# Block-diagonal gates, attention values and FFN sums of squares in fp32r passes over high and low parts, with the attention values gathered by block of keys

## The chip, the cores and the metric

The kernel runs on one core of one Trainium2 chip. The time is the device time of one execution in microseconds (us). The profile is one execution seen by the hardware profiler. TensorE appears in it as PE (matmuls) and PEld (its weight loads), VectorE as DVE, ScalarE as ACT, GpSimd as POOL, and SyncE, which issues most transfers, as SP.

## The reference, cut to what matters

A first block (convolution, a gated linear recurrence, stick-breaking attention, an MLP) is followed by two layers of a second block, on 512 positions of 1024 channels. The change is in the second block:

```python
def second_block(x, ...):
    for l in range(2):
        x = x + 0.5 * swiglu(rms_norm_2(x, ffn1_norm[l]), ...)          # 1024 -> 2816 -> 1024
        h = rms_norm_2(x, mix_norm[l])
        proj = h @ w_in[l] + b_in[l]
        q, k, v, f_logit, xr, gr, g_attn, g_rnn = jnp.split(proj, SPLIT_POINTS, axis=-1)
        q, k = rms_norm_2(q, q_norm[l]), rms_norm_2(k, k_norm[l])       # per head, 8 heads of 128
        log_f = jax.nn.log_sigmoid(f_logit)
        y_attn = forgetting_attention(q, k, v, log_f) @ w_o_attn[l]     # causal softmax(q k + c_i - c_j) v
        xr = causal_depthwise_conv(xr, conv_w[l], conv_b[l])            # 4 taps
        yr = rg_lru(xr, lru_w_a[l], lru_b_a[l], lru_w_x[l], lru_b_x[l], lru_lambda[l]) * gelu(gr)
        merged = sigmoid(g_attn) * y_attn + sigmoid(g_rnn) * (yr @ w_o_rnn[l])
        x = x + merged @ w_out[l]
        x = x + 0.5 * swiglu(rms_norm_2(x, ffn2_norm[l]), ...)

def rg_lru(x, w_a, b_a, w_x, b_x, lam):
    r = sigmoid(block_diag_linear(x, w_a, b_a))                         # 16 blocks of 64x64
    i = sigmoid(block_diag_linear(x, w_x, b_x))
    log_a = -8 * r * softplus(-lam); a = exp(log_a)
    u = sqrt(-expm1(2 * log_a)) * (i * x)
    # h_t = a_t h_{t-1} + u_t along the positions
```

## The kernel before, in words

Activations stand as tiles of 128 channels x 512 positions. Each large product is made of three fp32r passes over a high and a low part of both sides (`mm3`, L225 to L229): high x high, high x low, low x high. Weights come in chunks of 256 KB: `w` (L183 to L199) has SP load `raw`, ACT cast it to `hi` (L195) and DVE subtract for `lo` (L196), in rings of four. Sums grow in four PSUM banks, the tiles `a` (pool `pa`, four buffers); a new sum can begin only in a bank that has been read out. Four more banks serve small products: `xs` twice, `xm` and `xh` once each.

Small products use plain fp32 operands, for which PE executes two instructions where the program has one: the block-diagonal gates (L909, L910), the scores (L842), the values (L867) and the sums over partitions for the norms (`rows_of`, L270).

In a layer, `ffn` (L807), `mix` (L961) and `ffn` follow each other. The part of `mix` around the change runs in this order of the program:

- `stats`, and the block-diagonal matrices `bd`, loaded as fp32 (L988 to L995).
- Four pairs of sums give the eight tiles of xr. Each is scaled out of its bank into a tile `t` (L980, DVE) and moved with its bias into `xr` (L1004, ACT).
- `rnn` (L894), for each of eight tiles j: four taps of the convolution into `xc` on DVE (L905, L907); two gates on PE (L909, L910); on ACT tanh, tanh, exp, tanh and a square (L912 to L915, L298); two products on DVE (L918, L917). After j = 3 and after j = 7, ACT takes four square roots (L923) and DVE makes four products and four scans (L925, L926).
- The forget gate: one sum `fa` in an `a` bank (L1009 to L1013), read out by DVE into a tile `s` (L1016); then a softplus on ACT (L957 to L959), a scan, a transfer to DRAM.
- Twice, for half of the heads: the tokens of q, k and v. `tokens` (L255) needs four `a` banks at once, for the four blocks of 128 tokens, and takes each weight chunk through all four. Then `heads_T` (norm and transposes to `qkT`) for q and k, then `attn` (L870), and four tiles of the gelu branch.
- `attn_scores` (L836) makes the softmax rows of one block i of queries of one head in a tile `s`; `attn_values` (L856) transposes them into `xs`, copies to `pT` (L865), and multiplies with v for each block j of keys up to i, 128 columns at a time (L867).

A scheduler sets the order of each engine's instructions ahead of time; on the chip each engine takes its own in that order. Work marked with `hp()` goes ahead when it is ready. Pools give SBUF: a pool opened after another was closed takes the space of that one, and its first writers come behind the last readers of what lay there. Before, one pool `mb` (L966) holds the tiles for all of `mix`:

```python
self.pool(ctx, f"mb{l}", hm=8, t=3, bq=1, qk=5, v=6, qkT=8, cb=2, s=3, pT=2)   # L966
    pool = self.pool(c2, f"rn{l}", bd=4, xc=3, abc=8)                          # L986, closed after rnn
```

Of the kernel before, what the change touches and what calls it, by code (L numbers as in the profile page):

```python
# [7 lines left out]
F32 = mybir.dt.float32  # L8
F32R = mybir.dt.float32r
# [109 lines left out]
class Build:  # L119
# [96 lines left out]
        self.tc.keep_in_program_order(ins)  # L216
        return ins

    def split(self, src, tag):
        hi, lo = self.t(tag, F32R), self.t(tag, F32R)  # L220
        self.nc.scalar.copy(hi, src)
        self.nc.vector.tensor_tensor(lo, src, hi.bitcast(F32), op=OP.subtract)
        return hi, lo
# [42 lines left out]
    def rows_of(self, p, scale, xt="xm"):  # L266
# [4 lines left out]
                                  start=True, stop=True)  # L271
        return ps[:, 0:4]

    def rsqrt(self, src, w, g="m"):

        nc = self.nc
        m, r = self.small(w, g), self.small(w, g)
        nc.vector.tensor_scalar(m, src, EPS, None, op0=OP.add)
        nc.gpsimd.tensor_tensor(r, m, self.mhalf[:, :w], op=OP.pow)
        return r  # L280
# [8 lines left out]
        nc.scalar.copy(rb, ps)  # L289
        return rb  # L290

    def stats(self):
        rt = self.rsqrt(self.rows_of(self.p, 1.0 / D), 4)
        return rt, self.spread(rt)

    def square(self, x, tag="sq"):
# [12 lines left out]
    def setup(self):  # L309
        nc, cp = self.nc, self.cp  # L310
        self.cv = self.lined(cp, (128, NVEC), name="cv")
        with self.hp():
            nc.sync.dma_start(self.cv, self.ap["vecs"])
        cst = self.lined(cp, (128, 384), name="cst")
        nc.scalar.dma_start(cst, self.ap["cst"])
        self.ident = cst[:, 0:128]
        self.ones = {}
        for v, nm in ((1.0, "one"), (1.0 / D, "oned"), (1.0 / 512, "onec"), (1.0 / 128, "onev")):
            o = self.lined(cp, (128, 128 if v in (1.0, 1.0 / 512) else 2), name=nm)
            nc.gpsimd.memset(o, v)  # L320
            self.ones[v] = o
        self.mhalf = self.lined(cp, (128, 32), name="mhalf")
        nc.gpsimd.memset(self.mhalf, -0.5)
        self.cst = cst
# [482 lines left out]
    def ffn(self, n, l, nxt, spill=None):  # L807
        nc = self.nc
        h = self.hx
        with ExitStack() as ctx:  # L810
            self.pool(ctx, f"ffn{n}{l}", act=44, G=4)
            with self.hp():
                _, rb = self.stats()
            acts = []
            for f in range(0, 22, 2):
                accs = self.pairs(*[_cols(f"ffn{n}_w_{v}_2", l, 8, f * 128) for v in ("gate", "up")], h)
                ga, ua = accs[0:2], accs[2:4]
                for i in range(2):
                    with self.hp():
                        G, U = self.t("G"), self.t("G")  # L820
                        nc.vector.tensor_tensor(G, ga[i], rb, op=OP.mult)
                        nc.scalar.activation(G, G, AF.Silu)
                        nc.vector.tensor_tensor(U, ua[i], rb, op=OP.mult)
                        nc.vector.tensor_tensor(U, U, G, op=OP.mult)
                        acts.append(self.split(U, "act"))
            for m in range(0, 8, 2):
                for i, a in enumerate(self.pair(f"ffn{n}_w_down_2", l, 22, m * 128, acts)):
                    with self.hp():
                        x = self.x[m + i]
                        nc.vector.scalar_tensor_tensor(x, a, 0.5, x, op0=OP.mult, op1=OP.add)  # L830
                        if nxt:
                            self.ready(m + i, nxt, spill)
                        else:
                            nc.sync.dma_start(self.ap["oT"][(m + i) * 128:(m + i) * 128 + 128, :], x)
# [18 lines left out]
        nc.vector.tensor_scalar(s, s, ri, None, op0=OP.mult)  # L853
        return st

    def attn_values(self, st, v, vc, i, o):  # L856

        nc = self.nc
        n = (i + 1) * 128
        pt = self.aux("xs")  # L860
        for j in range(i + 1):
            js = slice(j * 128, j * 128 + 128)
            nc.tensor.transpose(pt[:, js], st[:, js], self.ident)  # L863
        pT = self.t("pT")
        nc.scalar.copy(pT[:, :n], pt[:, :n])  # L865
        for j in range(i + 1):
            nc.tensor.matmul(o[:, i * 128:n], v[j][:, vc:vc + 128], pT[:, j * 128:j * 128 + 128],  # L867
                             start=(i == 0 and j == 0), stop=(i == 3 and j == 3), skip_group_check=True)

    def attn(self, qT, kT, v, hd0, ct, cdram):  # L870

        nc = self.nc
        out, todo = [], []

        def values(st, hd, i):
            if i == 0:
                out.append(self.aux("xh"))
            self.attn_values(st, v, (hd - hd0) * 128, i, out[-1])
            if i == 3:
                y = self.t("x")  # L880
                nc.scalar.copy(y, out[-1])
                out[-1] = y

        for hd in range(hd0, hd0 + 4):
            cb = self.t("cb")
            nc.gpsimd.dma_start(cb, cdram[hd:hd + 1, :].to_broadcast([128, 512]))
            for i in range(4):
                todo.append((self.attn_scores(qT[hd - hd0], kT[hd - hd0], i, hd, ct, cb), hd, i))
                if len(todo) > 1:
                    values(*todo.pop(0))  # L890
        values(*todo.pop(0))
        return out

    def rnn(self, xr, bd, l, hb, sp4):  # L894
        nc = self.nc
        hs = []
        for j0 in range(0, 8, 4):
            av, vv, ix = [], [], []
            for j in range(j0, j0 + 4):
                xc = self.t("xc")  # L900
                for tap in range(CW2):
                    wv = self.col(("conv_w_2", l), j * CW2 + tap)
                    src = xr[j][:, tap:tap + 512]
                    if tap == 0:
                        nc.vector.tensor_scalar(xc, src, wv, self.col(("conv_b_2", l), j), op0=OP.mult, op1=OP.add)  # L905
                    else:
                        nc.vector.scalar_tensor_tensor(xc, src, wv, xc, op0=OP.mult, op1=OP.add)  # L907
                ga, gx = self.aux("xs"), self.aux("xs")
                nc.tensor.matmul(ga, bd[0][j // 4][:, j % 4], xc, start=True, stop=True)  # L909
                nc.tensor.matmul(gx, bd[1][j // 4][:, j % 4], xc, start=True, stop=True)  # L910
                ti, th, a = self.t("abc"), self.t("abc"), self.t("hm")
                nc.scalar.activation(th, ga, AF.Tanh, scale=0.5, bias=hb[:, j:j + 1])  # L912
                nc.scalar.activation(ti, gx, AF.Tanh, scale=0.5, bias=hb[:, 8 + j:9 + j])
                nc.scalar.activation(a, th, AF.Exp, scale=sp4[:, 8 + j:9 + j], bias=sp4[:, 8 + j:9 + j])
                nc.scalar.activation(th, th, AF.Tanh, scale=sp4[:, j:j + 1], bias=sp4[:, j:j + 1])  # L915
                a2 = self.square(a, "xc")
                nc.vector.scalar_tensor_tensor(th, a2, 1.0, th, op0=OP.add, op1=OP.mult)  # L917
                nc.vector.scalar_tensor_tensor(ti, ti, 1.0, xc, op0=OP.add, op1=OP.mult)  # L918
                av.append(a)
                vv.append(th)  # L920
                ix.append(ti)
# [39 lines left out]
    def mix(self, l):  # L961
        nc = self.nc
        h = self.hx
        with ExitStack() as ctx:
            lp = ctx.enter_context(self.tc.tile_pool(name=f"lp{l}", bufs=1))
            self.pool(ctx, f"mb{l}", hm=8, t=3, bq=1, qk=5, v=6, qkT=8, cb=2, s=3, pT=2)  # L966
            with self.hp():
                rt, rb = self.stats()
            hb = self.lined(lp, (128, 32), name="hb")
# [13 lines left out]
            ct = self.lined(lp, (128, 32), name="ct")  # L983
            cdram = self.dp.tile([8, 512], F32, name=f"cd{l}")
            with ExitStack() as c2:
                pool = self.pool(c2, f"rn{l}", bd=4, xc=3, abc=8)  # L986
                bd = []
                for nm in ("lru_w_a_2", "lru_w_x_2"):  # L988
                    b = [self.t("bd", shape=(128, 4, 128)) for _ in range(2)]
                    for hh in range(2):  # L990
                        nc.gpsimd.memset(b[hh], 0.0)
                        src = self.ap[nm][l, hh * 8:hh * 8 + 8].rearrange("(j two) c d -> two c j d", two=2)
                        nc.gpsimd.dma_start(b[hh][0:64, :, 0:64], src[0])
                        nc.gpsimd.dma_start(b[hh][64:128, :, 64:128], src[1])
                    bd.append(b)  # L995

                xr = []
                for m in range(0, 8, 2):
# [6 lines left out]
                        xr.append(u)  # L1005
                hs = self.rnn(xr, bd, l, hb, sp4)
                self.tap(f"hs{l}", hs[0])

            fa = self.acc()  # L1009
            for k0 in (0, 4):  # L1010
# [19 lines left out]
            for hf in range(2):  # L1030
                for n in range(3):
# [2 lines left out]
                    nc.gpsimd.dma_start(bq, self.ap["brow"][l:l + 1, c:c + 512].to_broadcast([128, 512]))  # L1034
                    ts = []
                    for tt, a in enumerate(self.tokens("w_in_2", l, c, h)):
                        v = self.t("v" if n == 2 else "qk")
                        with self.hp():
                            nc.vector.scalar_tensor_tensor(v, a, rt[:, tt:tt + 1], bq, op0=OP.mult, op1=OP.add)  # L1039
                        ts.append(v)  # L1040
                    if n == 0:
                        qT = self.heads_T(ts, 4, 128, qg)
                    elif n == 1:
# [142 lines left out]
```

## Time and profile before

| | us |
|---|---|
| median of 3 runs | 3426.9 (3426.14 to 3427.21) |
| the profiled execution's own time | 3427.6 |
| its span, first to last instruction | 3425.8 |
| PE busy with matmuls | 3390.9 |
| DVE busy | 1887.3 |
| ACT busy | 1309.0 |
| POOL busy | 165.2 |

The span is the stretch between the first and the last instruction of the profiled execution; its own time is what that execution is listed with. PE's matmuls are pipelined: a matmul's listed duration is longer than the step from its start to the next one's, and the step is what it costs in a row of matmuls.

### The profile page before, as it was taken

What the parts mean: (1) busy time and instruction counts of PE and PEld (TensorE: products, weight loads), DVE (VectorE), ACT (ScalarE), POOL (GpSimd) and SP (SyncE); (2) the same over time, 40 slices, a digit from 0 to 9 for tenths busy, and PEclk for the clock granted to TensorE, in tenths of its full rate; (3) what the DMA queues carried; (4) which work ended last, traced back from release to release, by engine and by line L of the source; (5) the groups of instructions that cost most, each with busy time, mean ns of one, the idle gap of its engine ahead of it and who ended that gap; (6) DMA issues with size and microseconds to landing.
All of it is one profiled execution on the core that took longest, in us unless ns stands there. A gap on an engine that the chain in (4) does not pass through costs nothing.

```text
span 3425.8 us, 42240 instructions
## 1 busy us (share of the span) xinstructions
PE 3390.9 (99%) x15436; PEld 2777.9 (81%) x15436; DVE 1887.3 (55%) x3164; ACT 1309.0 (38%) x2284; POOL 165.2 (5%) x273
## 2 busy tenths in 40 slices
PE   7999999999999999999999999999999999999999
PEld 6887778788888888788888888888887788888887
DVE  7698565544444434786455444444447865454442
ACT  3335443423333323654433333333336644343331
POOL 0011100000000001111000000000010110000000
PEclk9999999999999999999999999999999999999999
DMA  5223344333333333222333333333342232433332
GB/s 207 74 75 96 103 132 142 116 108 96 98 94 98 98 108 114 91 89 89 111 96 94 98 98 99 95 97 97 104 123 93 90 90 79 122 96 97 98 103 91
DMA packets 184064, 350.79 MB, mean 102 GB/s; under 512 B 21168, under 2 KB 22448, under 8 KB 182832
## 3 DMA queue, kind: packets, MB, share of 16 engines
q1 hardware_dynamic: 177552, 328.53, 31.4%
q0 software_dynamic: 6160, 19.37, 1.8%
q8 instruction: 121, 1.98, 0.2%
q14 instruction: 87, 0.71, 0.1%
q10 hardware_dynamic: 144, 0.20, 0.0%
HBM read 341.69 MB, written 6.32 MB: 102 GB/s over the span
## 4 chain that ended last, share of the span: by engine, by line
PE 97%; DVE 1%; ACT 1%; issue 0%; DMA 0%; POOL 0%; DVEq 0%; ACTq 0%; POOLq 0%
PE a L227 30%; PE a L229 30%; PE a L228 30%; PE xh L867 1%; PE xs L842 1%; PE xh L441 1%; PE xh L523 1%; PE xs L501 1%; PE xs L863 1%; PE xm L404 0%; DVE xc L907 0%; PE xh L517 0%; PE xh L330 0%; PE xh L480 0%; PE xs L909 0%
## 5 line engine op out<-in xcount | busy, mean ns | idle before, releaser
L196 DVE TENSOR_TENSOR lo<-raw,hi 128x512 fp32r<-128x512 f32 x1144 | 786.5, 689 | 1243.3 <-ACT hi L195 1228.9
L195 ACT CAST hi<-raw 128x512 fp32r<-128x512 f32 x1144 | 707.2, 619 | 1592.4 <-PE a L228 1299.1
L227 PE MATMUL a<-h,hi 128*128 128x512 f32 x2528 | 989.3, 393 | 2.3 <-ACT h L601 2.3
L228 PE MATMUL a<-h,hi 128*128 128x512 f32 x2528 | 991.1, 392 | 0.0
L229 PE MATMUL a<-h,lo 128*128 128x512 f32 x2528 | 982.9, 392 | 0.0
L227 PEld LDWEIGHTS a<-h,hi 128*128 128x128 f32 x2528 | 475.8, 188 | 107.4 <-issue 7.5
L229 PEld LDWEIGHTS a<-h,lo 128*128 128x128 f32 x2528 | 475.5, 188 | 103.3 <-issue 5.2
L228 PEld LDWEIGHTS a<-h,hi 128*128 128x128 f32 x2528 | 475.5, 188 | 102.9 <-issue 5.1
L228 PE MATMUL a<-act,hi 128*128 128x512 f32 x960 | 373.6, 389 | 0.0
L227 PE MATMUL a<-act,hi 128*128 128x512 f32 x960 | 373.5, 389 | 0.0
L229 PE MATMUL a<-act,lo 128*128 128x512 f32 x960 | 372.8, 389 | 0.0
L228 PE MATMUL a<-Y,hi 128*128 128x512 f32 x544 | 214.4, 394 | 0.0
L227 PE MATMUL a<-Y,hi 128*128 128x512 f32 x544 | 213.7, 393 | 0.0
L229 PE MATMUL a<-Y,lo 128*128 128x512 f32 x544 | 212.4, 391 | 0.0
L227 PEld LDWEIGHTS a<-act,hi 128*128 128x128 f32 x960 | 180.2, 188 | 37.5
L229 PEld LDWEIGHTS a<-act,lo 128*128 128x128 f32 x960 | 180.2, 188 | 37.4
L228 PEld LDWEIGHTS a<-act,hi 128*128 128x128 f32 x960 | 180.2, 188 | 37.4
L229 PE MATMUL a<-hi,h 128*128 128x512 f32 x512 | 204.3, 402 | 0.0
L228 PE MATMUL a<-lo,h 128*128 128x512 f32 x512 | 203.6, 398 | 0.0
L227 PE MATMUL a<-hi,h 128*128 128x512 f32 x512 | 199.6, 408 | 1.7 <-DVE qk L1039 1.7
L227 PEld LDWEIGHTS a<-Y,hi 128*128 128x128 f32 x544 | 102.1, 188 | 23.0 <-issue 1.6
L228 PEld LDWEIGHTS a<-Y,hi 128*128 128x128 f32 x544 | 102.1, 188 | 22.8 <-issue 1.8
(291 smaller groups left out, 3068.0 us busy)
## 6 DMA issues: line engine op xcount, KB each, us to landing
raw<-in_w_l SPq DMA_DIRECT2D x852, 256.0 KB, 2.6
raw<-in_w_first SPq DMA_DIRECT2D x284, 256.0 KB, 2.6
mr<-in_mod_b_ SPq DMA_DIRECT2D x64, 256.0 KB, 3.2
mq<-in_mod_a SPq DMA_DIRECT2D x8, 1024.0 KB, 8.5
xs<-x POOLq DMA_DIRECT2D x16, 256.0 KB, 2.3
cb<-cd POOLq DMA_DIRECT2D x16, 256.0 KB, 3.5
x<-xs POOLq DMA_DIRECT2D x16, 256.0 KB, 3.6
bq<-in_brow POOLq DMA_DIRECT2D x12, 256.0 KB, 3.8
```

Of the source, the lines that this page charges most:

```text
L195: nc.scalar.copy(hi, raw)
L196: nc.vector.tensor_tensor(lo, raw, hi.bitcast(F32), op=OP.subtract)
L227: mm(acc, w[0], x[0], start=start, stop=False)
L228: mm(acc, w[0], x[1], start=False, stop=False)
L229: mm(acc, w[1], x[0], start=False, stop=stop)
L441: mm(ps[:, i * 64:i * 64 + 64], k[:, s], q[:, s].rearrange("p (n c h) -> p n c h", c=2, h=h)[:, :, 1], start=True, stop=True)
L501: mm(z[:, o:o + n], q[pr, blk(i)], k[pr, :n], start=True, stop=True)
L523: mm(pt[pr, c], v[j][:, hd * 64:hd * 64 + 64], f[:, o + j * 128:o + j * 128 + 128], start=j == 0, stop=j == i, skip_group_check=True)
L842: nc.tensor.matmul(ps[:, :n], qT[:, ts], kT[:, :n], start=True, stop=True)
L863: nc.tensor.transpose(pt[:, js], st[:, js], self.ident)
L867: nc.tensor.matmul(o[:, i * 128:n], v[j][:, vc:vc + 128], pT[:, j * 128:j * 128 + 128], start=(i == 0 and j == 0), stop=(i == 3 and j == 3 ...
```

## The change

- Gates: `xc` is split into a high and a low part `xd` (ACT cast, DVE subtraction), the four `bd` matrices of a layer too, and each fp32 matmul of L909 and L910 is replaced by `mm3`.
- Values: a head's values are made at once, by block j of keys, for all blocks of queries from j on. One `mm3` of 512, 384, 256 and 128 columns takes the place of ten fp32 matmuls of 128 columns. The transposed rows are split into `pT` high and low, and v into high and low. The values of a head stand behind the first two blocks of scores of the next head.
- Sums of squares: in `ffn`, `stats(True)` splits `p` and makes eight fp32r matmuls with two columns for four fp32 ones with one column.
- Pools: `mb` has no `v`, `s` and `pT` any more, `t` goes from 3 to 2 and `cb` from 2 to 1. `rn` gets `bd=8` and `xd=4`. A new pool `at` with `v=8, s=5, pT=2` opens after `rn` has been closed.

```diff
+    def rows_of2(self, p, scale, xt="xm"):
+        hi, lo = self.split(p, "pr")
+        ps = self.aux(xt)
+        for i in range(4):
+            s = slice(i * 128, i * 128 + 128)
+            for n, part in enumerate((hi, lo)):
+                self.nc.tensor.matmul(ps[:, 2 * i:2 * i + 2], part[:, s], self.mean, start=n == 0, stop=n == 1)
+        return ps[:, 0:8:2]
...
-                _, rb = self.stats()
+                _, rb = self.stats(True)
...
-    def attn_values(self, st, v, vc, i, o):
-        n = (i + 1) * 128
-        pt = self.aux("xs")
-        for j in range(i + 1):
+    def attn_values(self, sts, v, vc):
+        o = self.aux("xh")
+        for j in range(4):
             js = slice(j * 128, j * 128 + 128)
-            nc.tensor.transpose(pt[:, js], st[:, js], self.ident)
-        pT = self.t("pT")
-        nc.scalar.copy(pT[:, :n], pt[:, :n])
-        for j in range(i + 1):
-            nc.tensor.matmul(o[:, i * 128:n], v[j][:, vc:vc + 128], pT[:, j * 128:j * 128 + 128],
-                             start=(i == 0 and j == 0), stop=(i == 3 and j == 3), skip_group_check=True)
+            n = 512 - j * 128
+            pt = self.aux("xs")
+            for i in range(j, 4):
+                nc.tensor.transpose(pt[:, (i - j) * 128:(i - j) * 128 + 128], sts[i][:, js], self.ident)
+            hi, lo = self.t("pT", F32R), self.t("pT", F32R)
+            nc.scalar.copy(hi[:, :n], pt[:, :n])
+            nc.vector.tensor_tensor(lo[:, :n], pt[:, :n], hi[:, :n].bitcast(F32), op=OP.subtract)
+            self.mm3(o[:, j * 128:], [a[:, vc:vc + 128] for a in v[j]], (hi[:, :n], lo[:, :n]), j == 0, j == 3)
...
         for hd in range(hd0, hd0 + 4):
+            sts = []
             for i in range(4):
-                todo.append((self.attn_scores(qT[hd - hd0], kT[hd - hd0], i, hd, ct, cb), hd, i))
-                if len(todo) > 1:
-                    values(*todo.pop(0))
-        values(*todo.pop(0))
+                sts.append(self.attn_scores(qT[hd - hd0], kT[hd - hd0], i, hd, ct, cb))
+                if i == 1 and todo:
+                    out.append(self.attn_values(*todo.pop(0)))
+            todo.append((sts, v, (hd - hd0) * 128))
+        out.append(self.attn_values(*todo.pop(0)))
...
                 ga, gx = self.aux("xs"), self.aux("xs")
-                nc.tensor.matmul(ga, bd[0][j // 4][:, j % 4], xc, start=True, stop=True)
-                nc.tensor.matmul(gx, bd[1][j // 4][:, j % 4], xc, start=True, stop=True)
+                xd = self.split(xc, "xd")
+                for g, b in ((ga, bd[0][j // 4]), (gx, bd[1][j // 4])):
+                    self.mm3(g, [v[:, j % 4] for v in b], xd, True, True)
...
-            self.pool(ctx, f"mb{l}", hm=8, t=3, bq=1, qk=5, v=6, qkT=8, cb=2, s=3, pT=2)
+            self.pool(ctx, f"mb{l}", hm=8, t=2, bq=1, qk=5, qkT=8, cb=1)
...
-                pool = self.pool(c2, f"rn{l}", bd=4, xc=3, abc=8)
+                pool = self.pool(c2, f"rn{l}", bd=8, xc=3, xd=4, abc=8)
...
-                    b = [self.t("bd", shape=(128, 4, 128)) for _ in range(2)]
+                    b = [self.t("abc", shape=(128, 4, 128)) for _ in range(2)]
...
-                    bd.append(b)
+                    bd.append([self.split(v, "bd", (128, 4, 128)) for v in b])
...
                 hs = self.rnn(xr, bd, l, hb, sp4)
                 self.tap(f"hs{l}", hs[0])
+            self.pool(ctx, f"at{l}", v=8, s=5, pT=2)
...
-                        v = self.t("v" if n == 2 else "qk")
+                        v = self.t("qk")
...
-                        ts.append(v)
+                            ts.append(self.split(v, "v") if n == 2 else v)
```

The change also moves instructions. The first place is PE in `mix` of the first layer, around the gates (`xs` are the banks of the gates, `a` those of the large sums, `xc` the convolved tile, `xd` its parts, `hi` and `lo` a weight chunk). Before, around the gates of j = 1 (L909, L910):

```order
L228 MATMUL a2441_11386<-lo2452_11428,h2199_10297 128x512
L229 MATMUL a2441_11386<-hi2451_11427,h2200_10298 128x512
L909 MATMUL xs2380_11168<-xc2379_11163,bd2296_10791 128x512
L910 MATMUL xs2381_11169<-xc2379_11163,bd2298_10799 128x512
L227 MATMUL a2440_11385<-hi2454_11445,h2203_10308 128x512
L227 MATMUL a2442_11387<-hi2445_11391,h2156_10075 128x512
```

With the change, from the last pass into `a2468`, the third bank of q, through what is left of the gates of j = 2 and the start of those of j = 3:

```order
L229 MATMUL a2468_11480<-hi2480_11538,h2206_10319 128x512
L228 MATMUL xs2401_11230<-xd2404_11233,bd2300_10809 128x512
L229 MATMUL xs2401_11230<-xd2403_11232,bd2301_10810 128x512
L228 MATMUL xs2402_11231<-xd2404_11233,bd2306_10825 128x512
L229 MATMUL xs2402_11231<-xd2403_11232,bd2307_10826 128x512
L227 MATMUL xs2410_11258<-xd2412_11260,bd2300_10809 128x512
L227 MATMUL xs2411_11259<-xd2412_11260,bd2306_10825 128x512
L228 MATMUL xs2410_11258<-xd2413_11261,bd2300_10809 128x512
```

and from the last gates, those of j = 7, to the next large sum:

```order
L227 MATMUL xs2446_11382<-xd2448_11384,bd2302_10813 128x512
L227 MATMUL xs2447_11383<-xd2448_11384,bd2308_10829 128x512
L228 MATMUL xs2446_11382<-xd2449_11385,bd2302_10813 128x512
L229 MATMUL xs2446_11382<-xd2448_11384,bd2303_10814 128x512
L228 MATMUL xs2447_11383<-xd2449_11385,bd2308_10829 128x512
L229 MATMUL xs2447_11383<-xd2448_11384,bd2309_10830 128x512
L227 MATMUL a2469_11481<-hi2471_11484,h2158_10085 128x512
```

Between the gates of j = 0 and those of j = 7 there stood 306 large passes and transposes of q and k; now there stand 60: 24 into the bank of `fa` and 12 into each of three banks of q. Of these, 36 come before the gates of j = 1, 12 between the parts of j = 1 and 12 between those of j = 2. From there to `a2469`, the fourth bank of q, PE has nothing but gates. The second layer has the same order.

The second place is DVE in the same stretch. Before, L1016 reads `fa` out right behind the convolution of j = 1:

```order
L196 TENSOR_TENSOR lo2452_11428<-raw2450_11425,hi2451_11427 128x512
L907 SCALAR_TENSOR_TENSOR xc2379_11163<-xr2317_10888,cv_72,xc2379_11163 128x512
L1016 TENSOR_TENSOR s2435_11365<-a2428_11328,rb2295_10778 8x512
L196 TENSOR_TENSOR lo2455_11446<-raw2453_11443,hi2454_11445 128x512
L980 TENSOR_TENSOR t2370_11138<-a2355_11060,rb2295_10778 128x512
```

With the change the same instruction is L1027, and it stands behind the last scan (now L936) of j = 7:

```order
L935 TENSOR_TENSOR abc2450_11394<-abc2450_11394,abc2451_11395 128x512
L936 SCALAR_TENSOR_TENSOR hm2443_11368<-hm2443_11368,abc2441_11366 128x512
L936 SCALAR_TENSOR_TENSOR hm2452_11396<-hm2452_11396,abc2450_11394 128x512
L1027 TENSOR_TENSOR s2461_11458<-a2454_11421,rb2297_10788 8x512
L1030 TENSOR_SCALAR s2461_11458<-s2461_11458,cv_72 8x512
L1031 TENSOR_TENSOR s2461_11458<-s2461_11458,s2462_11459 8x512
L196 TENSOR_TENSOR lo2484_11557<-raw2482_11554,hi2483_11556 128x512
```

Its tile `s` lies in the pool `at`, and so in the space of `rn`. `lo2484` is the fifth weight chunk of q; the chunk before it, `lo2481`, stands 62 rows earlier, and up to L1027 all rows between are of `rnn` but the two that read out the last two tiles of xr. On ACT the high part `hi2483` stands behind the softplus.

## Rows read from the trace of the kernel before

**Rows 1.** The page's first part: busy us (share of the span) and instructions of each engine.

```profile
span 3425.8 us, 42240 instructions
PE 3390.9 (99%) x15436; PEld 2777.9 (81%) x15436; DVE 1887.3 (55%) x3164; ACT 1309.0 (38%) x2284; POOL 165.2 (5%) x273
```

**Rows 2.** The waits, PE: line waited for, us in total, times, longest.

```profile
PE a L227 <- DVE qk L1039: 1.7, 2, 0.9
PE xm L404 <- ACT qkT L406: 0.8, 2, 0.4
```

**Rows 3.** Timeline of PE, first layer: start us, us, instruction, count.

```profile
1360.08 0.39 PE L229 MATMUL a<-h,lo 128*128 128x512 f32 x1
...
1361.44 0.39 PE L229 MATMUL a<-h,lo 128*128 128x512 f32 x1
...
1363.03 1.02 PE L909 MATMUL xs<-xc,bd 128*128 128x512 f32 x2
1363.89 1.02 PE L910 MATMUL xs<-xc,bd 128*128 128x512 f32 x2
1364.35 0.79 PE L227 MATMUL a<-h,hi 128*128 128x512 f32 x1
1364.98 0.40 PE L228 MATMUL a<-h,hi 128*128 128x512 f32 x1
```

**Rows 4.** Timeline of PE, values of one block of queries and scores.

```profile
1491.57 1.05 PE L867 MATMUL xh<-pT,v 128*128 128x128 f32 x8
1492.46 0.27 PE L863 MATMUL xs<-cst,s 128*128 128x128 f32 x1
1492.57 0.81 PE L842 MATMUL xs<-qkT,qkT 128*128 128x384 f32 x2
```

**Rows 5.** Timeline of all engines, sums of squares ahead of an `ffn`.

```profile
960.30 0.69 DVE L306 TENSOR_TENSOR p<-p,sq 128x512 f32<-128x512 f32 x1
...
965.34 0.95 PE L270 MATMUL xm<-oned,p 128*128 128x1 f32 x8
```

**Rows 6.** Page, costliest groups: DVE's subtraction and ACT's cast (busy, mean ns).

```profile
L196 DVE TENSOR_TENSOR lo<-raw,hi 128x512 fp32r<-128x512 f32 x1144 | 786.5, 689 | 1243.3 <-ACT hi L195 1228.9
L195 ACT CAST hi<-raw 128x512 fp32r<-128x512 f32 x1144 | 707.2, 619 | 1592.4 <-PE a L228 1299.1
```

**Rows 7.** Timeline of DVE in `rnn`, first layer.

```profile
1367.52 0.69 DVE L918 SCALAR_TENSOR_TENSOR abc<-abc,xc 128x512 f32<-128x512 f32 x1 [2.71 <-ACT abc L913]
...
1390.05 0.69 DVE L918 SCALAR_TENSOR_TENSOR abc<-abc,xc 128x512 f32<-128x512 f32 x1 [1.83 <-ACT abc L913]
1390.66 0.74 DVE L907 SCALAR_TENSOR_TENSOR xc<-xr,cv,xc 128x512 f32<-128x512 f32 x1
1391.32 0.69 DVE L917 SCALAR_TENSOR_TENSOR abc<-xc,abc 128x512 f32<-128x512 f32 x1
1391.92 0.75 DVE L907 SCALAR_TENSOR_TENSOR xc<-xr,cv,xc 128x512 f32<-128x512 f32 x1
...
1406.02 1.22 DVE L926 TENSOR_TENSOR_SCAN hm<-hm,abc 128x512 f32<-128x512 f32 x1
1407.15 0.67 DVE L925 TENSOR_TENSOR abc<-abc,abc 128x512 f32<-128x512 f32 x1
```

**Rows 8.** Timeline of ACT, first layer: softplus, gates of one tile, square roots.

```profile
1372.12 0.71 ACT L957 ACTIVATE s<-s,cv 8x512 f32<-8x512 f32 x1
...
1374.80 0.63 ACT L959 ACTIVATE s<-s 8x512 f32<-8x512 f32 x1
...
1387.91 0.69 ACT L912 ACTIVATE abc<-xs,hb 128x512 f32<-128x512 f32 x1 [0.87 <-PE xs L909]
...
1401.59 1.28 ACT L923 ACT_TABLE_LOAD   x1
1402.88 2.20 ACT L923 ACTIVATE abc<-abc 128x512 f32<-128x512 f32 x4
```

**Rows 9.** Windows: us; busy us of PE, PEld, DVE, ACT, POOL; granted clock; DMA.

```profile
600.00:609.00 9.00, 5.35 (x16) 3.99 (x17) 4.99 (x9) 3.24 (x5) 1.03 (x1) 0.50 0.17 64
1460.00:1540.00 80.00, 80.00 (x403) 66.04 (x403) 63.35 (x130) 41.69 (x90) 12.76 (x18) 1.00 0.30 93
```

More of the change, by code (lines that the diff above doesn't have):

```diff
@@ L217, in pin, with split @@
         return ins
-    def split(self, src, tag):
-        hi, lo = self.t(tag, F32R), self.t(tag, F32R)
+    def split(self, src, tag, shape=(128, 512)):
+        hi, lo = self.t(tag, F32R, shape), self.t(tag, F32R, shape)
         self.nc.scalar.copy(hi, src)
@@ L290, in spread, with stats @@
         return rb
-    def stats(self):
-        rt = self.rsqrt(self.rows_of(self.p, 1.0 / D), 4)
+    def stats(self, two=False):
+        rows = self.rows_of2 if two else self.rows_of
+        rt = self.rsqrt(rows(self.p, 1.0 / D), 4)
         return rt, self.spread(rt)
@@ L321, in setup @@
             self.ones[v] = o
+        self.mean = self.lined(cp, (128, 2), F32R, name="mean")
+        nc.scalar.copy(self.mean, self.ones[1.0 / D][:, 0:2])
         self.mhalf = self.lined(cp, (128, 32), name="mhalf")
@@ L810, in ffn @@
         with ExitStack() as ctx:
-            self.pool(ctx, f"ffn{n}{l}", act=44, G=4)
+            self.pool(ctx, f"ffn{n}{l}", act=44, G=4, pr=2)
             with self.hp():
-                _, rb = self.stats()
+                _, rb = self.stats(True)
             acts = []
@@ L854, in attn_scores @@
         return st
-    def attn_values(self, st, v, vc, i, o):
+    def attn_values(self, sts, v, vc):
         nc = self.nc
-        n = (i + 1) * 128
-        pt = self.aux("xs")
-        for j in range(i + 1):
+        o = self.aux("xh")
+        for j in range(4):
             js = slice(j * 128, j * 128 + 128)
-            nc.tensor.transpose(pt[:, js], st[:, js], self.ident)
-        pT = self.t("pT")
-        nc.scalar.copy(pT[:, :n], pt[:, :n])
-        for j in range(i + 1):
-            nc.tensor.matmul(o[:, i * 128:n], v[j][:, vc:vc + 128], pT[:, j * 128:j * 128 + 128],
-                             start=(i == 0 and j == 0), stop=(i == 3 and j == 3), skip_group_check=True)
+            n = 512 - j * 128
[6 more added lines that the diff above has]
+            self.mm3(o[:, j * 128:], [a[:, vc:vc + 128] for a in v[j]], (hi[:, :n], lo[:, :n]), j == 0, j == 3)
+        y = self.t("x")
+        nc.scalar.copy(y, o)
+        return y
     def attn(self, qT, kT, v, hd0, ct, cdram):
@@ L873, in attn @@
         out, todo = [], []
[L875 to L882, printed above, removed]
         for hd in range(hd0, hd0 + 4):
```

## The prediction

> **What bounds the kernel now.** I read the page's busy times first, then PE's waits, then the timelines of PE, DVE and ACT where the change lies. PE is busy 99% of the span [rows 1], and in `mix` it hardly waits: the two causes there come to 1.7 and 0.8 us over both layers [rows 2]. So two questions decide. What do the exchanged matmuls cost on PE? And does the new order still give PE something to do at every moment? The sum is made against the profiled execution's own 3427.6 us, 0.7 above the median of the runs.
>
> **Gates on PE.** A large fp32r pass of 512 columns costs 0.227 us: from 1360.08 to 1361.44 there are six steps [rows 3]. From the first gate at 1363.03 to 1364.98 there are two fp32 matmuls (four instructions) and one such pass: 1.95 less 0.23 is 1.72, or 0.86 each [rows 3]. Three passes cost 0.68. There are 8 tiles, 2 gates and 2 layers: 32 times 0.18, **5.8 us less**.
>
> **Values on PE.** Eight fp32 instructions of 128 columns take 0.89 us, 0.111 each [rows 4]; a head has twenty, 2.22. No row shows an fp32r pass narrower than 512. The cheap end is in proportion to the columns, but not under 0.111: 0.227, 0.170, 0.114 and 0.111, three times over, 1.87 a head, which saves 5.6 over 16 heads. The dear end is that a narrower pass is no faster than one fp32 instruction: two of 384 columns end 0.65 after the transpose before them, 0.325 each [rows 4], so 0.22 for 256 and 0.11 for 128. With 0.227 for the widest that is 2.64 a head, 6.7 more in all. I take the cheap end, **5.6 less**, since the one width that has a row is cheap, and keep both.
>
> **Sums of squares.** Eight instructions with a weight load each stay eight: 0. The split puts 0.62 and 0.69 [rows 6] between `p` and the sums. Before, `p` is ready at 960.99 and PE takes the sums at 965.34 [rows 5], so 4.3 us of other matmuls cover it. Without that cover it would be 1.3 in each of four `ffn`, 5 in all.
>
> **New work on DVE and ACT.** A layer gets 4 splits of `bd`, 8 of `xc`, 8 of v: 20 casts (12.4 us on ACT) and 20 subtractions (13.8 on DVE) [rows 6]. The low parts of `pT`, 1280 columns a head, are some 1.7 us each, 13.8 for 8 heads. In 1460 to 1540 DVE is busy 63.35 of 80 us [rows 9]; the free 16.6 take up what falls there. I count 0 for v and `pT`, and come back to this below. `xd` is another matter.
>
> **What is moved.** This term is the largest. In the order with the change, `fa` is read out of its bank behind the last scan, since its tile `s` now lies in the space of `rn`. Until then `fa` keeps one of the four banks, and q's tokens need all four. PE has 60 large passes after the gates of j = 0, and then nothing but gates until `a2469`. Four chunks of weights are held by the missing fourth sum, so no later one can be cast either. Undisturbed, PE would get through the 60, the 12 of `a2469` that these chunks allow, and 48 gate passes from 1363.03 in 120 times 0.227, 27.2 us: at 1390.3.
>
> How long `rnn` really takes is read from the steps. From the low part of one `xd` to that of the next:
> - two gate passes, their drain and the start, about 0.8 (0.227 twice, 0.39 less 0.23, two handovers);
> - ACT from its first tanh to the product on DVE: 1387.91 to 1391.32, 3.4 [rows 7, 8], 0.1 to start;
> - that product 0.6 and two taps of 0.66 [rows 7], 1.9;
> - the cast 0.6 and the subtraction 0.7, with 0.1 between.
>
> This makes 7.6 us, in which DVE and ACT mostly wait for each other. Five of the six steps from j = 1 to j = 7 are such. The one from j = 3 to j = 4 holds the square roots: 4.2 to the square, table load and first root 1.9 [rows 8], then four products of 0.6, one tap, three scans of 1.13 [rows 7] and the subtraction: 13.2. After j = 7 the same 6.1, four products and four scans (6.9), and L1016 with 0.7: 13.7. The low part of j = 1 is there by about 1375: the product of j = 0 at 1367.52 [rows 7], then ten steps and a table load. So `fa`'s bank is free at 1375 + 38 + 13.2 + 13.7 = 1440. Then PE has twelve passes, but the fifth chunk is cast only behind the softplus: 3.3 before, with a second table load 4.6 [rows 8], and 0.6 for the cast. PE runs on at about 1445, **55 us late**.
>
> The clock adds to it. At 600 to 609, where PE had waited for the sums of squares, the granted clock was 0.50, the level of 1.2 GHz [rows 9]. In the stall PE is busy 1.4 in 7.6, so I take the lower level: the two passes and the drain of each tile cost 0.6 more (4), and some 1.6 after the stall, as in those 9 us. The Trainium skill (TensorE: Matmul & The Clock Gate, "The HAM clock gate") says the same in its own terms: throttled is the default, and only activity lifts it. By that rule the sum stands; without it each layer would lose 55 and not 60, and the total would be 3524.
>
> **The sum.** 2 times 60, less 5.8, 5.6 and the 2.5 of old waits, is 106 more: 3427.6 + 106 = 3534, or 3533 on the scale of the median.
>
> Its bounds: if DVE never waited in `rnn`, its steps behind 1367.52 would still be 8 of 0.61 (L918), 7 convolutions of 2.44, 27 of 0.6 (L917, L925, the subtractions, xr) and 8 scans of 1.13: 47 us, `fa` free at 1415, PE on at 1420, 30 late. Both layers: 3473. If DVE and ACT took turns throughout, ACT's 42 (8 times 3.4, seven casts, eight roots, three table loads, three tiles of xr) come on top: 72 late, 77 with the clock, and with dear values 3580.
>
> **The rivals.**
> - *The stall is covered* (the other side): `fa` is read out before the scans, or PE has other sums to run. Then the exchange remains: 5.8 + 5.6 less, and 3416. What decides is where L1016 (now L1027) starts: before about 1381, when the 60 passes and the first gates are through, there is no loss. For it: before, it ran at the place of j = 1. Against it: the order of DVE, fixed ahead, has eight scans before it.
> - *DVE alone sets `rnn`'s pace*, and waits overlap better than I think: 30 to 45 late, 3473 to 3505.
> - *DVE becomes the bound in the attention too*: v and `pT` ask for 19.3 us a layer, beside stretches in which DVE is nearly full already; if a quarter to a half of it falls where no cover is, 10 to 20 in all: 3543 to 3553.
> - *The narrow passes are dear*: 12 more, 3545.
>
> **How the numbers follow.** The chain as worked out, alone or with some of the last two: 0.74. DVE's pace: 0.16. Turns throughout, beyond 3570: 0.05. Covered: 0.05. The range 3475 to 3580 takes in the bounds of the stall and of the values and leaves out the covered case and the far ends. A difference of about 0.2%, 7 us, can be told from none. Faster by more: 0.04, the covered case with cheap values; within it: 0.01; slower: 0.95.
>
> **What would show it.** Right: from about 1381 to 1445, and again in the second layer, a stretch of PE with gates alone, 7 to 8 us apart, the granted clock at 0.50, and PE's longest waits on `xd`; the read of `fa` behind the last scan; q's weight casts idle some 60 us. Gates in steps of 0.227 otherwise, and three passes in the values with steps that fall with the columns. Wrong: large passes between the gates of j = 3 to 7, or L1016's successor ahead of the scans; then the time is near 3416. If the tiles follow each other in under 5 us, DVE's pace is the right rival.

## The result and the profile after

The changed kernel takes 3559.8 us (median of 4 runs, 3558.6 to 3562.6) against 3426.5 for the kernel before in the same comparison: ratio 1.039, 95% interval 1.0375 to 1.0406, **133 us more**. 106 more were forecast, 3533, within 3475 to 3580. The profiled execution took 3562.61 us.

The page's first part after, which answers to [rows 1]; PE's granted clock in 40 slices of the span; and what the transfers moved in them:

```profile
span 3559.6 us, 42203 instructions
PE 3413.3 (96%) x15340; PEld 2788.1 (78%) x15340; DVE 1948.5 (55%) x3272; ACT 1338.5 (38%) x2329; POOL 155.6 (4%) x273
...
PEclk9999999999999998899999999999996999999999
...
GB/s 199 72 78 107 96 168 98 122 104 98 95 98 98 102 124 42 71 95 89 107 92 97 96 97 98 95 98 96 109 113 9 107 89 92 107 95 95 99 103 92
```

PE has 96 instructions fewer and is busy 22 us longer, in a span that is 134 longer. No engine's busy time explains this. Two dips do, one in each layer: the transfers fall to 42 and 9 GB/s, and the clock falls with them. PE's waits after (line waited for, us in total, times, longest), where before no cause in `mix` came to more than 1.7 [rows 2]:

```profile
PE xs L227 <- ACT xd L221: 76.8, 12, 7.8
PE a L227 <- DVE s L1027: 24.6, 2, 12.3
...
PE xs L228 <- DVE xd L222: 5.2, 2, 2.6
...
PE a L227 <- ACT Y L221: 2.6, 2, 1.3
```

The timeline of PE after, first layer, of the gates the first high and the first low pass of each tile from the low part of j = 1 on (start us, us, instruction, count, idle time before it and its releaser):

```profile
1377.27 0.39 PE L228 MATMUL xs<-xd,bd 128*128 128x512 f32 x1
...
1384.81 1.22 PE L227 MATMUL xs<-xd,bd 128*128 128x512 f32 x2 [6.47 <-ACT xd L221]
1385.83 0.63 PE L227 MATMUL a<-hi,h 128*128 128x512 f32 x1
...
1389.84 0.39 PE L228 MATMUL xs<-xd,bd 128*128 128x512 f32 x1
...
1397.38 1.22 PE L227 MATMUL xs<-xd,bd 128*128 128x512 f32 x2 [6.47 <-ACT xd L221]
1398.40 0.63 PE L228 MATMUL xs<-xd,bd 128*128 128x512 f32 x1
...
1411.96 0.79 PE L228 MATMUL xs<-xd,bd 128*128 128x512 f32 x1 [2.61 <-DVE xd L222]
...
1421.83 0.63 PE L228 MATMUL xs<-xd,bd 128*128 128x512 f32 x1
...
1430.19 0.63 PE L228 MATMUL xs<-xd,bd 128*128 128x512 f32 x1
...
1438.56 0.63 PE L228 MATMUL xs<-xd,bd 128*128 128x512 f32 x1
...
1452.77 0.80 PE L227 MATMUL a<-hi,h 128*128 128x512 f32 x1 [12.30 <-DVE s L1027]
...
1458.00 1.19 PE L227 MATMUL a<-hi,h 128*128 128x512 f32 x4 [0.31 <-ACT hi L195]
```

This is the stall of the prediction. From 1390 to 1452 PE has nothing but gates (1381 to 1445 was forecast), and a large sum begins again only when L1027 has read `fa` out of its bank. The timeline of DVE after, behind the last gates, shows it behind the last two scans:

```profile
1449.60 2.33 DVE L936 TENSOR_TENSOR_SCAN hm<-hm,abc 128x512 f32<-128x512 f32 x2
1452.04 0.68 DVE L1027 TENSOR_TENSOR s<-a,rb 8x512 f32<-8x512 f32 x1
```

Windows of the stall after (us; busy us of PE, PEld, DVE, ACT, POOL; granted clock; DMA share; GB/s):

```profile
1400.00:1420.00 20.00, 3.60 (x7) 1.66 (x6) 14.57 (x20) 12.07 (x18) 0.10 (x1) 0.50 0.00 0
1420.00:1440.00 20.00, 8.32 (x18) 5.33 (x18) 9.85 (x16) 8.79 (x14) 0.00 (x0) 0.50 0.00 0
1480.00:1600.00 120.00, 119.48 (x559) 97.14 (x558) 84.03 (x163) 57.46 (x108) 14.25 (x21) 1.00 0.33 98
```

The granted clock is at its lower level of 1.2 GHz, and no byte of weights is loaded. DVE and ACT mostly wait for each other: DVE is busy 14.6 and 9.9 of 20 us, ACT 12.1 and 8.8. Behind the stall, PE is busy 119.5 of 120 us at the full clock, and DVE, busy 84, has room in spite of the new work.

### The profile page after: what moved, and what is told of

It reads as the page before. It is cut to its first block, busy times and chain, and to the rows that moved or that the text cites. A ratio compares the mean times of both kernels' runs of the same rounds, so it can differ in the third digit from the quotient of the medians.

```text
span 3559.6 us, 42203 instructions
## 1 busy us (share of the span) xinstructions
PE 3413.3 (96%) x15340; PEld 2788.1 (78%) x15340; DVE 1948.5 (55%) x3272; ACT 1338.5 (38%) x2329; POOL 155.6 (4%) x273
## 4 chain that ended last, share of the span: by engine, by line
PE 95%; DVE 2%; ACT 2%; issue 0%; DMA 0%; POOL 0%; SPq 0%; ACTq 0%; DVEq 0%; POOLq 0%
PE a L227 29%; PE a L228 29%; PE a L229 29%; PE xs L855 1%; PE xh L454 1%; PE xh L536 1%; PE xs L514 1%; DVE xc L916 1%; PE xs L227 1%; PE xs L878 0%; DVE hm L936 0%; PE xm L417 0%; PE xs L228 0%; ACT hm L924 0%; PE xs L229 0%
## 5 line engine op out<-in xcount | busy, mean ns | idle before, releaser
L195 ACT CAST hi<-raw 128x512 fp32r<-128x512 f32 x1144 | 707.7, 619 | 1610.7 <-PE a L228 1248.2
L227 PEld LDWEIGHTS a<-hi,h 128*128 128x128 f32 x512 | 97.5, 192 | 50.2 <-DVE s L1027 26.1
L227 PEld LDWEIGHTS a<-Y,hi 128*128 128x128 f32 x544 | 102.9, 190 | 26.9 <-ACT Y L221 2.9
```

Source lines behind the costliest of these rows:

```text
L195: nc.scalar.copy(hi, raw)
L227: mm(acc, w[0], x[0], start=start, stop=False)
```

## The experiments

Ratios are to the kernel before, timed in the same comparison (3425.3 to 3427.1 us). "Excess" is added up over PE's matmuls in a run's profiled execution: the step from a matmul's start to the next one's, less the usual step of that line and width. It counts waits and steps at the lower clock alike. It is 45 us in the kernel before and 188 after.

| run | us | ratio and interval |
|---|---|---|
| after, `fa` in `qkT` (e1) | 3463.9 | 1.0108 (1.0093 to 1.0123) |
| before, `v`, `s`, `pT` in the late pool (e2) | 3524.5 | 1.0289 (1.0272 to 1.0306) |
| e1, fp32 gates (e3) | 3445.0 | 1.0053 (1.0038 to 1.0068) |
| e1, values as before (e4) | 3479.2 | 1.0155 (1.0139 to 1.0170) |
| e1, `s` by block (e5) | 3465.4 | 1.0113 (1.0098 to 1.0128) |
| e3, `s` by block (e6) | 3447.2 | 1.0060 (1.0045 to 1.0075) |
| e6, `t` 3 and `qk` 4 (e7) | 3454.6 | 1.0083 (1.0066 to 1.0100) |
| e6, fp32 sums of squares (e8) | 3447.0 | 1.0058 (1.0043 to 1.0073) |
| e2, `fa` in `qkT` (e9) | 3452.9 | 1.0077 (1.0060 to 1.0094) |
| e6, `t` 3, one wide `s` (e10) | 3444.9 | 1.0055 (1.0040 to 1.0070) |
| e10, last head ahead (e11) | 3445.9 | 1.0058 (1.0043 to 1.0073) |
| e10, `v` back in `mb`, `pT` by width (e13) | 3425.0 | 0.9995 (0.9986 to 1.0004) |

**The forget gate's tiles outside the space of `rn` (e1).**

```diff
-            fz, fe, fc = [self.t("s")[0:8] for _ in range(3)]
+            fz, fe, fc = [self.t("qkT")[0:8] for _ in range(3)]
```

> The changed kernel, but the three tiles of the forget gate (fz, fe, fc) come from the buffers of qkT, which lie in the pool that is open throughout, and not from the new pool in the space of rnn. Theory A (the forget gate's read-out waits for the end of rnn and so keeps one of the four banks): the stall of some 66 us a layer goes, the exchange of fp32 for three passes shows as 11 us less, the waits near the end of mix (4.6 and 5.8 us) stay or shrink: 3413 to 3425 us. Theory B (the splits load DVE and ACT, and rnn is slow for that, wherever the tile lies): still over 3520. Theory C (two tiles t for three, so that the last sums of xr keep their banks): still over 3520.

Measured 3463.9: 96 of the 133 us come back with one word changed. In the timeline of DVE of this run the read-out stands where it stood before the change, at j = 1:

```profile
1369.33 0.67 DVE L1027 TENSOR_TENSOR qkT<-a,rb 8x512 f32<-8x512 f32 x1
```

The stall with gates alone is gone. But 37 us over the kernel before are left, where the exchange should have shown as a gain.

**The pools alone, with none of the new arithmetic (e2).** On the kernel before:

```diff
-            self.pool(ctx, f"mb{l}", hm=8, t=3, bq=1, qk=5, v=6, qkT=8, cb=2, s=3, pT=2)
+            self.pool(ctx, f"mb{l}", hm=8, t=3, bq=1, qk=5, qkT=8, cb=2)
...
+            self.pool(ctx, f"at{l}", v=6, s=3, pT=2)      # opened after rnn
```

> The kernel before with one edit: v, s and pT are moved from the pool of all of mix into a pool opened after rnn. No splits, no other passes, t stays at 3. Theory A: nearly the whole loss appears without any of the new arithmetic; the steps of rnn lack a cast and a subtraction (1.4 us) but have slower gates, so 45 to 65 us a layer: 3515 to 3560. Theories B and C: within 10 us of 3427.

Measured 3524.5, 97 more than before. The fp32 gates stand in the same stall, and PE waits for the convolution in place of `xd`:

```profile
PE xs L909 <- DVE xc L907: 40.1, 10, 6.4
PE a L227 <- DVE s L1017: 23.2, 2, 11.6
```

So most of the loss is the place of three tags in SBUF.

**Gates in fp32 (e3).** On e1, the gates as before the change, with no split of `xc` and `bd`:

```diff
-                xd = self.split(xc, "xd")
-                for g, b in ((ga, bd[0][j // 4]), (gx, bd[1][j // 4])):
-                    self.mm3(g, [v[:, j % 4] for v in b], xd, True, True)
+                nc.tensor.matmul(ga, bd[0][j // 4][:, j % 4], xc, start=True, stop=True)
+                nc.tensor.matmul(gx, bd[1][j // 4][:, j % 4], xc, start=True, stop=True)
...
```

> As e1_fa_tiles, but the gates stay fp32 matmuls, without the splits of the convolved tile and of the block-diagonal matrices. If the gates' passes are worth what their steps say (0.86 for 0.68 us, 32 times), this is 5.8 us above e1_fa_tiles; if DVE is short of time in rnn there, less than that or even below it.

Measured 3445.0, 19 less than e1, where the passes alone are 5.8 cheaper on PE. In e1 the timeline of PE shows why: ahead of the gates of j = 2 it waits for the cast of `xc` and then runs at half speed, 0.43 a step:

```profile
1382.86 1.22 PE L227 MATMUL xs<-xd,bd 128*128 128x512 f32 x2 [4.90 <-ACT xd L221]
1383.88 0.63 PE L227 MATMUL a<-hi,h 128*128 128x512 f32 x1
1384.31 0.63 PE L228 MATMUL a<-lo,h 128*128 128x512 f32 x1
```

The excess is 92 in e1 and 67 in e3; less the 5.8, that is the 19. Of the 25 some 9 lie here, in both layers together, and some 12 at the end of `mix`, where the last head comes later; the rest is spread over the attention. Why the splits delay the last head was not taken apart.

**Values as before (e4).** On e1, one `attn_values` for each block of queries, with fp32 `v` (L1054 reads v out of its banks straight into `v`):

```diff
...
-            self.pool(ctx, f"at{l}", v=8, s=5, pT=2)
+            self.pool(ctx, f"at{l}", v=6, s=3, pT=2)
...
-                        v = self.t("qk")
+                        v = self.t("v" if n == 2 else "qk")
...
```

> As e1_fa_tiles, but the values are made as before, block by block of queries in fp32, v and the transposed rows unsplit. By their steps the new values are worth about 6 us on PE (2.22 for 1.82 us a head), so this would be 6 above e1_fa_tiles; if the waits near the end of mix (10 us together) come from the last head's values standing late, they go here and it is some 4 below.

Measured 3479.2, 15 above e1, but not because the old values are dear. PE's longest wait in `mix` is a new one, with an excess of 19 and 18 us around it, and the timeline of DVE has the four read-outs of v in one piece, behind the scans:

```profile
PE a L227 <- DVE v L1054: 19.6, 2, 9.8
```
```profile
1478.56 2.73 DVE L1054 SCALAR_TENSOR_TENSOR v<-a,m,bq 128x512 f32<-128x512 f32 x4
```

It is `fa`'s stall once more, now with all four banks. As a price of the values the run is inconclusive. It shows one thing more: PE's wait for `Y` is not among its waits, as it is not in e2, which has the old values too; so that wait comes with the new values.

**Scores by block of queries (e5 on e1, e6 on e3).** At this point I held the five whole `s` to be what makes the last head, and so `Y`, late.

```diff
-        st = self.t("s")
+        st = self.t(f"s{i}", shape=(128, n))
...
-            self.pool(ctx, f"at{l}", v=8, s=5, pT=2)
+            self.pool(ctx, f"at{l}", v=8, s0=2, s1=2, s2=2, s3=2, pT=2)
```

> The changed kernel with the forget gate's tiles in `qkT` (as in the run that gave 3463.87) and with the attention scores in a pair of buffers for each block of queries (128 to 512 columns wide, 10 KB a partition together, as the five of 512 before). Theory A: with five whole buffers a head's scores can't be begun before the transposes of the head before it, so that the eight heads come some 33 us apart instead of 23, the last head's values are late, and TensorE stands before `Y` at the end of the mix (excess steps of about 11 us in the first layer and 10 in the second). Then the wait goes and the time falls by 12 to 21, to 3443 to 3452. Theory B: the new values (two casts and three passes for each block of keys) are late by themselves: within 4 us of 3464.

> The same pair of buffers for each block of queries, on the kernel whose gates are fp32 again (which gave 3444.99). Theory A: the late last head cost about 5 us a layer there, so 3432 to 3440. Theory B: within 4 us of 3445.

Nothing moved: 1.0113 against 1.0108, and 1.0060 against 1.0053. The wait for `Y` stayed in both. That theory fell.

**A third `t`, paid for with a `qk` (e7), and fp32 sums of squares (e8), both on e6.**

```diff
-            self.pool(ctx, f"mb{l}", hm=8, t=2, bq=1, qk=5, qkT=8, cb=1)
+            self.pool(ctx, f"mb{l}", hm=8, t=3, bq=1, qk=4, qkT=8, cb=1)      # e7
```
```diff
-                _, rb = self.stats(True)
+                _, rb = self.stats()      # e8, in ffn
```

> The kernel of the run before this one with three `t` buffers and four `qk` as the kernel before has nearly (three and five). Theory: what is left over the kernel before in the stretch of the scans and the queries (about 7 us a layer) comes from the third `t` given up, so 3418 to 3430. Rival: it comes from `qk` and `cb` or from order alone: within 4 us of the run before this one, or above it.

> The kernel of the second run of this call with the sums of squares of the feed-forward's norm as fp32 products again. Theory: the split is hidden or equal, as forecast: within 2 us of that run. Rival: the split and the eight passes stand on the chain before the feed-forward, 1 to 2 us each of the two times: 2 to 4 us less than that run.

e7 is 7.5 slower than e6: PE waits 9.3 us for `qkT` and 8.2 for `qk`, against 0.6 and 4.0 in e6, so `qk` is the scarcer of the two. e8 equals e6 within noise (1.0058, 1.0060): no cost of the sums of squares shows, as forecast.

**The pools alone, with `fa` in `qkT` (e9).** The edit of e1, on e2.

> The kernel before with only `v`, `s` and `pT` in a pool opened after the scans (which gave 3524.46, 97 above the kernel before), and with the forget gate's tiles in `qkT` in place of `s`. Theory A: the whole loss by the pool goes through the forget gate's bank; then it is the kernel before again, 3424 to 3430. Rival: `v` and `s`, which wait for the same space, still cost: 3432 to 3450.

Measured 3452.9: some 70 of the 97 us go through `fa`, and 27 stay. The rival was right, with v, though 2.9 above its range. First the kernel before, then e9, in the timeline of DVE of the first layer:

```profile
1452.49 1.44 DVE L1039 SCALAR_TENSOR_TENSOR v<-a,m,bq 128x512 f32<-128x512 f32 x2 [1.54 <-PE a L229]
...
1457.72 1.22 DVE L926 TENSOR_TENSOR_SCAN hm<-hm,abc 128x512 f32<-128x512 f32 x1
```
```profile
1461.26 2.33 DVE L926 TENSOR_TENSOR_SCAN hm<-hm,abc 128x512 f32<-128x512 f32 x2
1463.62 2.73 DVE L1040 SCALAR_TENSOR_TENSOR v<-a,m,bq 128x512 f32<-128x512 f32 x4
```

Before, v's last read-outs stand ahead of the last four scans; in e9, behind them. PE has waited 4.2 us for `qkT` at 1458; its next sum starts at 1464.43 after 5.6 us more, and its steps are 0.43 until 1469.

**A third `t` without loss of a `qk` (e10), and the last head ahead (e11).**

```diff
-            self.pool(ctx, f"mb{l}", hm=8, t=2, bq=1, qk=5, qkT=8, cb=1)
+            self.pool(ctx, f"mb{l}", hm=8, t=3, bq=1, qk=5, qkT=8, cb=1)
...
-            self.pool(ctx, f"at{l}", v=8, s0=2, s1=2, s2=2, s3=2, pT=2)
+            self.pool(ctx, f"at{l}", v=8, s0=2, s1=2, s2=2, s3=1, pT=2)
```
```diff
-        out.append(self.attn_values(*todo.pop(0)))
+        with self.hp():      # e11, on e10
+            out.append(self.attn_values(*todo.pop(0)))
```

> The kernel with fp32 gates and scores by block (3447.16) with three `t` again and `qk` left at five; the room comes from the second buffer of the widest scores. Theory: with two `t` the read-out of xr's and the gelu's sums is held up, and this is the 7 us a layer that PE loses between 1380 and 1460; then 3431 to 3437. Rival: something else in that stretch; within 3 us of 3447.

> The run before this one with the values of the last head of each half set ahead of the other work by the scheduler (`hp`). Theory: the last head's transposes stand between large passes for 13 us though the softmax rows were ready at 1720.3, and so its value sums end at 1736.4 and PE waits for `Y`; set ahead they end by about 1727, the wait goes, and the time falls by 8 to 12. Rival: the chain of two casts and three passes for each of four blocks is what takes the time; within 3 us of the run before this one.

e10 is 2 below e6, where its theory had 10 to 16: two `t` in place of three cost about nothing. e11 told nothing of its theory: the setting moved no instruction on any engine, so it is e10 a second time, 0.9 away. The timelines of e10, DVE and then PE, show what is left around 1460:

```profile
1461.85 1.21 DVE L935 TENSOR_TENSOR_SCAN hm<-hm,abc 128x512 f32<-128x512 f32 x1
1462.98 2.04 DVE L1049 SCALAR_TENSOR_TENSOR qk<-a,m,bq 128x512 f32<-128x512 f32 x3
```
```profile
1463.76 0.79 PE L227 MATMUL a<-h,hi 128*128 128x512 f32 x1 [1.18 <-DVE qk L1049]
1464.36 0.63 PE L228 MATMUL a<-h,hi 128*128 128x512 f32 x1
```

With the new values v goes through `qk` before it is split. Three of its four read-outs stand behind three scans here too: the `qk` tiles they need still hold k, whose last transposes PE takes at 1459.28.

**`v` outside the space of the scans (e13).**

```diff
-            self.pool(ctx, f"mb{l}", hm=8, t=3, bq=1, qk=5, qkT=8, cb=1)
+            self.pool(ctx, f"mb{l}", hm=8, t=3, bq=1, qk=5, qkT=8, v=8, cb=1)
...
-            self.pool(ctx, f"at{l}", v=8, s0=2, s1=2, s2=2, s3=1, pT=2)
+            self.pool(ctx, f"at{l}", s0=2, s1=2, s2=1, s3=1, pT=2, pU=2)
...
-            hi, lo = self.t("pT", F32R), self.t("pT", F32R)
+            pw = {"tag": "pT"} if j < 2 else {"tag": "pU", "shape": (128, 256)}
+            hi, lo = self.t(dt=F32R, **pw), self.t(dt=F32R, **pw)
...
-                        v = self.t("qk")
+                        v = self.t("x" if n == 2 and hf == 0 else "qk")
```

> The kernel of the last two runs (3444.9) with two edits. One: `v` high and low lie in `mb` again, outside the space of the scans, and v's first four tokens are read into `x` tiles in place of `qk`. Two: the parts of `pT` for the two narrow blocks of keys get tiles of their own, so that the casts of one block needn't wait for the passes of the block before. Theory: what is left is the same mechanism once more, v's read-outs held behind the scans (here by `qk` tiles that wait for k's transposes and for v's split), some 6 us a layer at 1460, and a chain of four blocks in turn through one pair of `pT`, some 4 to 5 us a layer at 1740; both go, 3420 to 3428, and PE's waits on `qk` fall to those of the kernel before (1.7 in all) and that on `Y` vanishes. Rival for the first: the stretch is short of work whatever holds the banks; then the waits at 1460 stay, 3432 to 3438. Rival for the second: the four blocks are late because their transposes stand late in PE's order; then the wait on `Y` stays and 8 to 9 us with it.

Measured 3425.0 (11 runs), 20 less than e10. In the timeline of DVE the read-outs of v, now into `x`, stand ahead of the last four scans again:

```profile
1453.11 1.40 DVE L1050 SCALAR_TENSOR_TENSOR x<-a,m,bq 128x512 f32<-128x512 f32 x2
...
1458.17 1.22 DVE L936 TENSOR_TENSOR_SCAN hm<-hm,abc 128x512 f32<-128x512 f32 x1
```

PE's waits in `mix` are those of the kernel before [rows 2]:

```profile
PE a L227 <- DVE qk L1050: 1.7, 2, 0.9
PE xm L417 <- ACT qkT L419: 0.8, 2, 0.4
```

The wait on `Y` is gone too; the excess is 46. Both rivals fell. The two edits came in one run; in e10 the excess at the two places was 6.6 to 8 us a layer (1.7 of it as before) and 4 to 5, so v has the larger share.

## Why the prediction was right, and where it was short

**The mechanism held, step by step.** L1016's successor stands behind the last scan; gates alone in between; the longest waits on `xd`; the granted clock at 0.50, one of the two levels named. One sign was off in size: the casts of q's weights (L195) stand still from 1371.5 to 1457.3, 86 us where some 60 were forecast. e1 and e2 show the cause from both sides: the late pool without the new arithmetic costs 97, and `fa` taken out of it gives 96 back.

**The stall was mis-sized, by 7 to 8 us a layer.** The prediction had low parts 7.6 us apart, 13.2 over the square roots, and 13.7 to the end, and the 0.6 of the clock apart. The timeline gives, from 1377.27, 12.6, 8.6, 13.6, 9.9, 8.4, 8.4, and 14.2 to the end of L1027 at 1452.7. The last two plain steps are 7.6 and the clock's 0.6, within 0.2. What failed is "five of the six steps are such" and the start at 1375: I counted the twelve large passes that stand between the high and the low passes of j = 1, and the twelve of j = 2, as work that fills PE's wait. They stand on the chain, since the low passes come behind them in PE's order: those of j = 2 at 1389.84, four us after the large ones began at 1385.83, most of them at half speed. That step is 5 too long, four of them by these passes. The start is 2.3 late for the same reason. The step behind the square roots took 9.9, since ACT loads a table once more ahead of the next tanh (timeline of ACT), which the 7.6 did not hold:

```profile
1413.26 1.28 ACT L922 ACT_TABLE_LOAD   x1 [5.18 <-PE xs L229]
```

PE ran on at 1458.0 where 1450 (1445 and the 5 for the clock) was forecast: 16 in both layers. By the excess, 133 us in the two stretches against the 120 forecast, it is 13.

**A term that was missing:** the wait for `Y` near the end of `mix`. The last head's four blocks of keys can start only behind its last scores, and each takes its turn through one pair of `pT`; with a second pair, in e13, where v was moved too, the wait is gone. PE runs dry and starts again at half speed: 4.6 and 5.8 us of excess, some 10 in all. The stall's 13 to 16 and these 10 are 23 to 26 of the 27 us short.

**The exchange on PE.** The values fell as in the cheap end: in e13 a head's passes add up to 0.68, 0.53, 0.36 and 0.27 us for the four widths, 1.84 against 2.22. The timeline of PE after shows widths of 384 and 128:

```profile
1546.50 0.33 PE L228 MATMUL xh<-pT,v 128*128 128x384 f32 x1
1546.67 0.34 PE L229 MATMUL xh<-pT,v 128*128 128x384 f32 x1
1546.84 0.27 PE L878 MATMUL xs<-cst,s 128*128 128x128 f32 x1
...
1558.58 0.22 PE L228 MATMUL xh<-pT,v 128*128 128x128 f32 x1
1558.64 0.27 PE L229 MATMUL xh<-pT,v 128*128 128x128 f32 x1
1558.75 1.29 PE L855 MATMUL xs<-qkT,qkT 128*128 128x512 f32 x4
```

The steps are 0.17 and, for 128, 0.06 and 0.11: they fall with the columns, and "the narrow passes are dear" falls. Yet the time doesn't show the 5.6. e13, which has this exchange and no new wait, is 1.3 us below the kernel before by the medians and 2.7 by the spans, and its interval, 0.9986 to 1.0004, takes in no difference at all. Added up by line in the two profiled executions, the values lose some 6 and the other 512-column passes gain some 3; executions of one kernel lie as far apart (2.8 us in e13's eleven, 3.4 in the fifteen beside them). The gates' 5.8 was right as a count of passes but not as a saving. Where the tiles of `rnn` follow each other closely, the split is on the chain; e3, without it, is 19 us faster and has some 9 us less excess at this place. That the gates could pay with `fa` and `v` both read ahead of the scans was not tried.

**The rivals.** "Covered" fell. "DVE sets the pace" fell: steps of 8.4, not under 5. "DVE becomes the bound in the attention" fell: PE busy 119.5 of 120 us. "Turns throughout", 77 late, was not reached: 1458.0 is 68 behind 1390.3. The zero for the sums of squares held (e8).

**The clock.** The Trainium skill (TensorE: Matmul & The Clock Gate, "What's actually happening") has the throttled state as the default that activity lifts. The traces agree: the granted clock is 0.50 in the stall, where PE is busy 3.6 and 8.3 of 20 us, and 1.00 in 1480 to 1600.

## What to carry to other kernels

In this kernel, opening a pool in freed space was a move of instructions: each first writer went behind the last reader of what lay there, and where that writer read a PSUM bank, as with `fa` and v, TensorE paid. So for each tag that goes into a late pool, ask which bank its first write frees and who waits for the bank; `fa` cost 70 to 96 us, `v` up to 27, and `s` and `pT`, in the late pool in e13 too, nothing that shows. And in a stall, count what stands in the engine's order between two steps of the chain: it is no filler but part of it.

## What was not expected of the hardware

A short wait cost more than itself: in e10, after 1.45 and 1.18 us of waiting, the granted clock was 0.50 from 1464 to 1469 and the steps stayed at 0.43, some 2.8 us on top. And a saving on narrow passes may have been partly given back: in e13 the values take some 6 us less on PE, and the 13,680 large passes of 512 columns some 3 more. That stands on one execution of each kernel, no wait in the profile explains it, and no run shows that the narrow passes are its cause.
